# Output projections of both attentions in two halves of the contraction, in a two-layer trunk on one core

## The chip, the cores and the metric

One core of a Trainium2 chip runs the whole program. The metric is the device time of one execution in microseconds (us). The kernel before took 1870.69 us as the median of three runs (1869.51, 1870.69 and 1877.07).

## What is computed

Two layers, each a macaron: half a SwiGLU feed-forward, an attention, half a SwiGLU feed-forward, every one behind an RMS norm and added to the stream x (512 tokens x 1024). Layer 0 has a stick-breaking attention with 16 heads of 64, layer 1 a sliding-window attention with 16 query heads, 2 key heads and sinks. What the change touches is the end of each attention:

```python
x = x + stick_breaking_attention(h, sb_w_in, sb_w_out)
x = x + sliding_window_attention(h, positions, sw_w_in, sw_w_out, q_gain, k_gain, sinks)
...
    return o @ w_out          # o: 512 x 1024 (16 heads of 64), w_out: 1024 x 1024
```

## The kernel before, in words

The stream is kept transposed in SBUF as eight tiles `x0` to `x7` of 128 features x 512 tokens. Everything on TensorE is done in split precision: each operand is a rounded high part and a low part (`oh`, `ol` and so on), and one product of a 128x128 weight tile with a 128x512 operand is three matmuls (`terms`, L214). Such a group of three is called a term below. All TensorE instructions have line 85, since one wrapper records them; the tile names tell them apart. (So have VectorE's where it is held in program order.)

Weights come from DRAM in units of 512 KB (eight 128x128 tiles). SyncE issues the load into a `raw` buffer (L296, three buffers), ScalarE casts it to the high part (L345) and VectorE subtracts to get the low part (L350) into a `slot` (three buffers; a feed-forward has two more of each, `rawx` and `slotx`). `queue` sets the order of the units, and `pump` starts the next load or split when `used` has counted a slot's eight tiles down to zero.

The order of an attention is written by hand. `_Filler` (L101) is a generator of steps with a cost; `fill.run(cost)` between the small steps of a head pair puts that much matmul work there. The amounts are tables: `FILL` and `RATE` for the first attention (L41, one RATE a head pair, two more for its end), `WFILL` and `WRATE` for the second. TensorE keeps the order in which it is written; VectorE and ScalarE are reordered by a scheduler when the program is built, except in the first units of a feed-forward, where `order(True)` holds VectorE in program order too.

The filler of an attention first makes queries, keys and values, then turns to `project_early` (L800): three output tiles of the projection are opened, each in a PSUM bank of the `mm` ring (three banks), and each takes the next head pair's output as soon as it is there (`settled`). An output tile needs all eight 128-row parts of `o`, so the banks and the three weight slots under them stay taken until the last head pair is through. When the last scores are done, a fourth tile is opened in a PSUM bank that has come free; its weights are split into two old query or key tiles (`spare`, `advance`, L355; in the trace `qsw` and `ksw`, or `qw`). `project_out` (L819) finishes the open tiles and does the other four; after each, `residual` (L474) adds it to `x` on VectorE, and `norm_tile` prepares the next feed-forward: a cast on ScalarE (`xh`, L432), a subtraction on VectorE (`xl`, L433), a square on ScalarE, and its sum in `acc` on GpSimd or, for the last two, VectorE (L441). After tile 3 of the first attention `rope_tables` (L886) puts some fifty small VectorE instructions and a sine and a cosine on ScalarE between them.

The feed-forward behind it starts with `plain` (L499). TensorE goes through unit 0 (`gu`, eight terms, one for each x tile); then come the row sums (`ss`, `norm_rows`, with a chain of small VectorE steps that ends in `nr`), unit 1, and the broadcast of the norm (`bc`, `norm_bcast`), whose operand `dg` ScalarE makes from `nr` (L468). The sums of x for the later products (`xg` L506, `t` and its cast L513) are made by ScalarE and VectorE beside it.

## Time and profile before

| | |
|---|---|
| median of three runs | 1870.69 us |
| profiled execution, its whole time | 1871.98 us |
| profiled execution, span | 1870.2 us |
| instructions | 29257 |
| mean granted TensorE clock | 0.989 |
| VectorE busy | 1503.5 us (80%) |
| ScalarE busy | 938.3 us (50%) |
| GpSimd busy | 98.6 us (5%) |
| DMA | 170.94 MB, mean 91 GB/s |
| first attention's projection, first to last matmul | 570.3 to 629 us |
| second attention's projection, first to last matmul | 1426.2 to 1518 us |

Times in the profile are counted from the start of the span. In a row of the timeline the first number is the start, the second the time from there to the row's end, and a bracket at the end gives the idle time of the engine just ahead and what ended it. In a row of the windows view, each engine has its busy time and, in brackets, its instructions; the third number from the end is the granted TensorE clock as a share of full speed.

### The profile page before, as it was taken

To read this page: it belongs to the slowest core of one execution; us is meant where nothing else is said; L and a number is where in the kernel's file an instruction comes from. 1 tells how busy PE (TensorE), PEld (TensorE's weight loads), DVE (VectorE), ACT (ScalarE), POOL (GpSimd) and SP (SyncE) were. 2 spreads that over 40 slices of the span, in tenths; PEclk is the share of its full clock that TensorE was granted. 3 is DMA by queue.
4 is the path that set the end of the run, shared out by engine and by line. 5 is a ranking of instruction groups with operands and counts; after the bars stand their busy time and mean duration, and the time that the engine had idled before them with its cause. 6 is when DMAs were issued, how large, how long until landed. Compare 5 with 4: busy or idle time off the path is not lost.

```text
span 1870.2 us, 29257 instructions
## 1 busy us (share of the span) xinstructions
PE 1827.5 (98%) x11730; PEld 1646.9 (88%) x11730; DVE 1503.5 (80%) x2450; ACT 938.3 (50%) x1497; POOL 98.6 (5%) x83
## 2 busy tenths in 40 slices
PE   7999999999999999999999999999999999999999
PEld 5999999878887789999988999999887788999997
DVE  8888888668987988888869888787688588888884
ACT  6444444456765644444446444444457564444441
POOL 1000000100000100000010000000252210000000
PEclk8999999999999999999999999999999899999999
DMA  5333333221121332333323233322220043333331
GB/s 169 102 102 102 102 102 102 71 77 57 57 68 37 133 101 91 113 94 109 97 74 120 96 100 104 113 92 91 72 68 25 12 134 102 102 102 102 102 102 57
DMA packets 48808, 170.94 MB, mean 91 GB/s; under 512 B 5792, under 2 KB 6048, under 8 KB 48672
## 3 DMA queue, kind: packets, MB, share of 16 engines
q1 hardware_dynamic: 48672, 169.07, 28.3%
q8 instruction: 92, 1.51, 0.3%
q14 instruction: 44, 0.36, 0.1%
HBM read 166.96 MB, written 2.10 MB: 90 GB/s over the span
## 4 chain that ended last, share of the span: by engine, by line
PE 81%; DVE 11%; ACT 4%; issue 3%; POOL 1%; DMA 0%; SPq 0%; ACTq 0%; POOLq 0%; DVEq 0%
PE dn L85 25%; PE a L85 23%; PE c L85 11%; PE b L85 6%; PE tok L85 3%; PE op L85 3%; PE gu L85 3%; DVE keep L732 1%; PE pv L85 1%; DVE t L85 1%; PE q L85 1%; PE k L85 1%; DVE slot L350 1%; PE z L85 1%; PE sc L85 1%
## 5 line engine op out<-in xcount | busy, mean ns | idle before, releaser
L85 PE MATMUL dn<-hs,slot 128*128 128x512 f32 x1152 | 279.1, 391 | 0.0
L85 PEld LDWEIGHTS dn<-hs,slot 128*128 128x128 f32 x1152 | 211.1, 188 | 40.3
L85 PE MATMUL dn<-hs,slotx 128*128 128x512 f32 x960 | 234.2, 392 | 3.3 <-DVE hs L85 1.8
L345 ACT CAST slot<-raw 128x1024 fp32r<-128x1024 f32 (+1 forms) x155 | 160.0, 1033 | 147.0 <-PE a L85 55.2
L85 PE MATMUL a<-t,slot 128*128 128x256 f32 x1728 | 230.2, 283 | 0.0
L85 PEld LDWEIGHTS a<-t,slot 128*128 128x128 f32 x1728 | 222.7, 191 | 6.6
L85 PEld LDWEIGHTS dn<-hs,slotx 128*128 128x128 f32 x960 | 175.5, 188 | 38.4 <-ACT hs L482 2.7
L350 DVE TENSOR_TENSOR slot<-raw,slot 128x1024 fp32r<-128x1024 f32 (+1 forms) x141 | 173.8, 1234 | 16.4 <-ACT slot L345 16.4
L474 DVE SCALAR_TENSOR_TENSOR x<-dn,x 128x512 f32<-128x512 f32 x192 | 131.8, 687 | 44.8 <-PE dn L85 44.7
L85 PEld LDWEIGHTS a<-t,slotx 128*128 128x128 f32 x1008 | 131.1, 191 | 5.3
L85 PE MATMUL a<-t,slotx 128*128 128x256 f32 x1008 | 134.2, 283 | 0.0
L85 PE MATMUL b<-xh,half 128*128 128x256 f32 x608 | 121.9, 283 | 0.0
L441 POOL TENSOR_TENSOR acc<-acc,sq 128x512 f32<-128x512 f32 x30 | 44.9, 1496 | 1313.3 <-ACT sq L440 1313.3
L85 PE MATMUL tok<-slot,xh 128*128 128x256 f32 x576 | 110.9, 292 | 0.1
L85 PEld LDWEIGHTS b<-xh,half 128*128 128x128 f32 x608 | 100.4, 192 | 0.0
L345 ACT CAST slotx<-raw 128x1024 fp32r<-128x1024 f32 x64 | 66.8, 1050 | 64.9 <-PE a L85 56.7
L345 ACT CAST slot<-rawx 128x1024 fp32r<-128x1024 f32 x60 | 63.1, 1052 | 69.4 <-PE a L85 43.3
L85 PE MATMUL c<-xh,slot 128*128 128x256 f32 x480 | 96.2, 283 | 0.0
L85 PEld LDWEIGHTS tok<-slot,xh 128*128 128x128 f32 x576 | 89.9, 192 | 3.3 <-issue 1.1
L553 DVE TENSOR_TENSOR g<-c,r 128x256 f32<-128x256 f32 x76 | 32.3, 424 | 74.7 <-PE c L85 74.1
L85 PE MATMUL gu<-xh,slot 128*128 128x512 f32 x256 | 86.3, 408 | 3.8 <-ACT slot L345 1.9
L547 ACT COPY r<-a 128x256 f32<-128x256 f32 x152 | 56.1, 369 | 65.2 <-PE a L85 64.7
(360 smaller groups left out, 4149.3 us busy)
## 6 DMA issues: line engine op xcount, KB each, us to landing
raw<-in_w_dram SPq DMA_DIRECT2D x165, 512.0 KB, 3.5
rawx<-in_w_dram SPq DMA_DIRECT2D x96, 512.0 KB, 3.5
raw<-in_sbqk_dram SPq DMA_DIRECT2D x16, 512.0 KB, 3.5
raw<-in_swin_dram SPq DMA_DIRECT2D x10, 512.0 KB, 3.5
raw<-in_sbv_dram SPq DMA_DIRECT2D x8, 512.0 KB, 3.5
raw<-in_sbo_dram SPq DMA_DIRECT2D x8, 512.0 KB, 3.5
raw<-in_swo_dram SPq DMA_DIRECT2D x8, 512.0 KB, 3.5
x<-in_xt_dram SPq DMA_DIRECT2D x8, 256.0 KB, 5.2
```

The source lines that it names most:

```text
L85: return self._tc.keep_in_program_order(method(*args, **kwargs))
L345: nc.scalar.copy(hi, src)
L350: nc.vector.tensor_sub(lo, src, hi)
L441: (nc.gpsimd if k < POOL_SQUARES else nc.vector).tensor_add(self.acc, self.acc, sq)
L474: self.nc.vector.scalar_tensor_tensor(self.x[n], ps, factor, self.x[n], ALU.mult, ALU.add)
L547: nc.scalar.copy(r, ps)
L553: nc.vector.tensor_add(g[:, W2:], ps, self.cells["r6", f])
L732: nc.vector.tensor_tensor_scan(rev, rev, rev, 1.0, ALU.mult, ALU.bypass)
```

## The change

The contraction of the output projection is cut in two. `opened` now goes through sixteen half tiles: with parts 0 to 3 of `o` all eight output tiles, each added to `x` at once, then with parts 4 to 7 all eight again, with a second addition and then the norm. `project_early` retires a first-half tile as soon as its four terms are done and opens the next, so three are open until the second half is reached; the extra PSUM bank is taken only then. A unit of `w_out` is laid out as two output tiles x four parts, in the order of use, and no unit is split into old query tiles any more. `residual` thus runs 16 times an attention and not 8; matmuls, weight loads and DMAs are as many as before. Three fill rates are other numbers: RATE for the last head pair 0.54 to 0.95, two of WRATE 1.0 and 0.76 to 1.3 each.

```diff
-RATE = (1.05, 1.05, 1.1, 1.06, 1.05, 1.05, 0.99, 0.54, 1.46, 4.8)
+RATE = (1.05, 1.05, 1.1, 1.06, 1.05, 1.05, 0.99, 0.95, 1.46, 4.8)
...
-WRATE = (1.79, 0.32, 0.71, 0.75, 1.46, 1.0, 0.76, 1.88, 2.19, 2.26)
+WRATE = (1.79, 0.32, 0.71, 0.75, 1.46, 1.3, 1.3, 1.88, 2.19, 2.26)
...
+    def open_out(self, opened, bank=None):
+        h, n = divmod(self.outs, KD)
+        self.outs += 1
+        opened.append([h, n, self.bank("op") if bank is None else bank, self.take(HALF), 0])
+
+    def project_terms(self, t, parts, last):
+        h, n, ps, w, at = t
+        for k in range(at, last):
+            t[4] = k + 1
+            yield from self.terms(ps, [(w[k], parts[h * HALF + k])], first=(k == 0), last=(k == HALF - 1))
...
-            if self.spare and len(opened) == UNITS:
-                bank, tiles = self.spare()
-                self.advance(*tiles)
-                opened.append([bank, self.take(KD), 0])
-            ready = [t for t in opened if t[2] < self.settled]
+            if self.spare and opened[0][0]:
+                self.open_out(opened, self.spare())
+                self.spare = None
+            ready = [t for t in opened if t[4] < min(HALF, self.settled - t[0] * HALF)]
...
+            yield from self.project_terms(t, parts, t[4] + 1)
+            if t[0] == 0 and t[4] == HALF:
+                self.residual(t[1], t[2], 1.0)
+                opened.remove(t)
+                self.open_out(opened)
...
     def project_out(self, parts, opened, following):
+        while opened or self.outs < 2 * KD:
+            if not opened:
+                self.open_out(opened)
+            t = opened.pop(0)
+            for _ in self.project_terms(t, parts, HALF):
+                pass
+            h, n = t[:2]
+            self.residual(n, t[2], 1.0)
+            if h:
+                following(n)
+            if h and n == UNITS and not self.roped:
                 self.rope_tables()
...
-                    net.queue(aps["sbo"][n], special=(n == UNITS))
+                    net.queue(aps["sbo"][n])
...
+    a["sbo"] = c(np.asarray(sb_w_out).reshape(2, HALF, P, HALF, 2, P).transpose(0, 3, 2, 4, 1, 5)).reshape(KD, P, KD * P)
```

What this does to the order is seen at three places. The first is ScalarE in the feed-forward behind the first attention, up to the norm's diagonal `dg`. Before:

```order
L506 ACTIVATE xg<-x_111,gain 128x512
L506 ACTIVATE xg<-x_112,gain 128x512
L345 CAST half_6416<-rawx_6240 128x512
L345 CAST slot_6291<-raw_6221 128x1024
L468 ACTIVATE dg<-ident,nr 128x128 x4
```

And now (line 960 is line 942 of before, the sine of the rope tables):

```order
L345 CAST half_6431<-rawx_6255 128x512
L345 CAST slot_6306<-raw_6236 128x1024
L960 ACT_TABLE_LOAD
L960 ACTIVATE sin<-ang 128x4x8
L962 ACTIVATE cos<-t 128x4x8
L506 ACTIVATE xg<-x_113,gain 128x512
L506 ACTIVATE xg<-x_114,gain 128x512
L345 CAST slot_6358<-rawx_6250 128x1024
L513 CAST t_6319<-t 128x1024
L513 CAST t_6329<-t 128x1024
L468 ACTIVATE dg<-ident,nr 128x128 x4
```

The rope tables, two `xg`, a weight cast and two casts of `t` now stand ahead of `dg`; before, all of these but the rope's, which had run earlier, stood behind it. On TensorE `bc` is where it was, right behind unit 1.

The second place is ScalarE in the last head pair of the first attention, where the values of the pair ahead (`pv`) are folded. Before:

```order
L726 ACTIVATE keep<-z 128x2x384
L790 COPY fold<-pv 64x512
L728 ACTIVATE beta<-z 128x2x384
L790 COPY fold<-pv 64x512
L754 CAST wt_5781<-tr 128x4x128
```

Now:

```order
L726 ACTIVATE keep<-z 128x2x384
L345 CAST slot_5754<-raw_5452 128x1024
L728 ACTIVATE beta<-z 128x2x384
L790 COPY fold<-pv 64x512 x2
L754 CAST wt_5799<-tr 128x4x128
```

A weight cast, which the earlier release of the slot brings here, and `beta` now stand ahead of the first fold.

The third place is TensorE late in the second attention, from the end of one block's values (`pv`) through the transposes of its probabilities (`ptr`) to the next scores (`sc`). Before:

```order
L85 MATMUL pv<-ph,v 128x256
L85 MATMUL ptr<-ident,e 128x128 x4
L85 MATMUL sc<-kh_13436,qs_14534 128x256 x2
L85 MATMUL sc<-kl_13437,qs_14534 128x256 x2
L85 MATMUL sc<-kh_13436,qs_14596 128x256 x2
L85 MATMUL sc<-kl_13437,qs_14596 128x256 x2
L85 MATMUL pv<-ph,v 128x256
```

Now:

```order
L85 MATMUL pv<-ph,v 128x256
L85 MATMUL ptr<-ident,e 128x128 x4
L85 MATMUL op<-oh_14222,slot_14367 128x512
L85 MATMUL op<-ol_14223,slot_14367 128x512
L85 MATMUL op<-oh_14222,slot_14367 128x512
L85 MATMUL op<-oh_13860,slot_14665 128x512
L85 MATMUL op<-ol_13861,slot_14665 128x512
L85 MATMUL op<-oh_13860,slot_14665 128x512 x2
L85 MATMUL op<-ol_13861,slot_14665 128x512
L85 MATMUL op<-oh_13860,slot_14665 128x512
L85 MATMUL op<-oh_14222,slot_14665 128x512
L85 MATMUL op<-ol_14223,slot_14665 128x512
```

Projection matmuls now stand between transposes and scores, where none stood. Over the whole window stage 40 of the 64 terms are ahead of the last `pv`, and 24 were; in the first attention 27 are ahead of the last pair's `pvs`, and 18 were.

More of the change, by code (lines that the diff above doesn't have):

```diff
@@ L814, in project_early @@
             t = ready[0]
[L815 to L825 removed]
+            yield from self.project_terms(t, parts, t[4] + 1)
[3 more added lines that the diff above has]
+                self.open_out(opened)
+    def project_out(self, parts, opened, following):
+        while opened or self.outs < 2 * KD:
+            if not opened:
+                self.open_out(opened)
+            t = opened.pop(0)
[6 more added lines that the diff above has]
+            if h and n == UNITS and not self.roped:
                 self.rope_tables()
@@ L847, in spare @@
             def spare():
[L848 to L849 removed]
+                return self.psum.tile([P, T], F32, tag="pv", name="op", bufs=1)
             for p in range(PAIRS):
@@ L1168, in spare @@
             def spare():
-                tiles = [ap.tile([P, KD * P], F32R, tag="q", name="qw", bufs=2) for _ in range(2)]
-                return self.psum.tile([P, 2, T], F32, tag="z", name="op", bufs=1)[:, 0, :], tiles
+                return self.psum.tile([P, 2, T], F32, tag="z", name="op", bufs=1)[:, 0, :]
             for u in range(CHUNKS * TB + 4):
```

21 lines of the change are left out of this document (4 added, 17 removed).

## The prediction

> **What bounds the kernel now.** I read the page's busy shares first, then TensorE's waits in the two stretches that the change touches, then the granted clock there.
>
> ```profile
> PE 1827.5 (98%) x11730; PEld 1646.9 (88%) x11730; DVE 1503.5 (80%) x2450; ACT 938.3 (50%) x1497; POOL 98.6 (5%) x83
> ```
>
> TensorE is busy for 98% of the span and the change takes no matmul away. So it can only win back time in which TensorE stands still, or runs slowly. The waits of TensorE, first from 560 to 680 us (last head pairs, projection, start of the next feed-forward), then from 1426 to 1520 us (the second attention's end); columns are total us, times, longest:
>
> ```profile
> PE pv L85 <- DVE o L791: 2.9, 1, 2.9
> PE gu L85 <- ACT xh L432: 1.7, 1, 1.7
> PE dn L85 <- ACT hs L482: 0.8, 1, 0.8
> PE dn L85 <- DVE hs L85: 0.7, 1, 0.7
> PE gu L85 <- DVE xl L433: 0.5, 1, 0.5
> ```
>
> ```profile
> PE pv L85 <- DVE pl L1104: 2.5, 4, 1.3
> PE ptr L85 <- DVE pl L1104: 1.9, 1, 1.9
> PE qtr L85 <- DVE pl L1104: 1.4, 1, 1.4
> PE qtr L85 <- DVE hf L975: 0.5, 1, 0.5
> PE op L85 <- ACT oh L1113: 0.5, 1, 0.5
> ```
>
> That is 6.6 us and 6.8 us of standing still. The clock adds to the second (the windows view; the number after POOL's is the granted clock):
>
> ```profile
> 1445.00:1450.00 5.00, 4.51 (x20) 3.80 (x18) 4.91 (x15) 3.73 (x11) 1.56 (x1) 0.66 0.13 23
> 1450.00:1455.00 5.00, 3.58 (x15) 2.93 (x16) 3.76 (x15) 3.12 (x10) 1.77 (x2) 0.70 0.22 85
> 1455.00:1460.00 5.00, 5.00 (x25) 4.73 (x25) 2.02 (x9) 3.08 (x11) 1.50 (x2) 0.62 0.00 0
> 1470.00:1475.00 5.00, 3.67 (x16) 3.04 (x16) 3.88 (x17) 4.09 (x15) 1.76 (x2) 0.74 0.00 2
> 1475.00:1480.00 5.00, 5.00 (x29) 4.28 (x28) 1.72 (x4) 2.21 (x7) 2.82 (x2) 0.91 0.02 3
> ```
>
> Five times (1 - clock) gives 1.7 + 1.5 + 1.9 = 5.1 us lost to a lower clock in the first three rows and 1.3 + 0.45 = 1.75 us in the last two. Each dip stands right behind a wait:
>
> ```profile
> 1444.74 0.78 PE L85 MATMUL qtr<-ident,q 128*128 128x128 f32 x4 [1.42 <-DVE pl L1104]
> 1451.41 0.66 PE L85 MATMUL ptr<-ident,e 128*128 128x128 f32 x4 [1.90 <-DVE pl L1104]
> 1471.47 0.39 PE L85 MATMUL pv<-pl,v 128*128 128x256 f32 x1 [1.33 <-DVE pl L1104]
> ```
>
> So what can be won is 6.6 us at the first attention and 6.8 + 6.85 us at the second, 20 us or 1.1% at the very most.
>
> **The change part by part.** One term and one addition cost:
>
> ```profile
> 604.91 0.39 PE L85 MATMUL op<-o4h,qsw 128*128 128x512 f32 x1
> 605.59 0.39 PE L85 MATMUL op<-o5h,qsw 128*128 128x512 f32 x1
> L474 DVE SCALAR_TENSOR_TENSOR x<-op,x x16: 674/684/692, 603.7 to 1518.3; 128x512 f32<-128x512 f32 x16
> ```
>
> A term is 605.59 - 604.91 = 0.68 us of TensorE. An addition is 0.68 us of VectorE; eight more in each attention are 5.5 us there, none of it on TensorE unless a bank or a later VectorE step waits. Splits of weights, DMAs and SyncE's issues are as many as before and in the same order; they move earlier, into the last head pairs, where the slots now come free.
>
> *Second attention.* Before, three tiles times four finished parts are 12 terms; then the filler is empty, and TensorE goes from values to transposes to scores with nothing between (the third place in the order). Now 32 first-half terms are there. The wait of 1.42 at 1444.74 and the dip behind it (a third of the first 5.1, 1.7) stay: the order up to there is the same. Before 1451.41 there is one term more (0.68), and the split into `qw` on VectorE (1.2 by its neighbours of the same size) is gone from ahead of `pl`: 1.90 becomes 0.3, so -1.6, and the two dip stretches behind it go, 5.1 - 1.7, so -3.4. At 1471.47 three to four terms stand ahead: -1.3, and its dip, -1.75. Against this: the last two transposes have no term between them any more (+0.7, a term), and 5.5 us of additions and three more weight splits fall into the stretch on VectorE. VectorE is 3.76 and 2.02 of 5 us busy in the rows 1450 to 1460, so most of it fits; I take +0.8, with ends of 0 and 4.0 (the three waits above, put back). Sum: -1.6 - 3.4 - 1.3 - 1.75 + 0.7 + 0.8 = -6.6 us.
>
> *First attention, last head pair.* The wait of 2.9 is for the fold of the pair ahead; its rows:
>
> ```profile
> 577.53 1.50 PE L85 MATMUL pv<-wt,v 128*128 128x512 f32 x8
> 579.40 0.81 ACT L726 ACTIVATE keep<-z 128x768 f32<-128x768 f32 x1 [2.26 <-DVE beta L733]
> 580.84 0.81 ACT L728 ACTIVATE beta<-z 128x768 f32<-128x768 f32 x1
> 582.68 1.51 PE L85 MATMUL pv<-wt,v 128*128 128x512 f32 x8 [2.90 <-DVE o L791]
> ```
>
> More filler is ahead of the first `pv` (two terms, 1.36 us), but ScalarE now has a weight cast (about 1.0) and `beta` (0.81) between `keep` and the fold, and VectorE a split and `beta` ahead of `o` (about 2.0 together). 2.9 + 2.0 - 1.36 is 3.5: the wait stays, +0.6. Ends: -2.9 (gone) and +2.0 (nothing of the filler helps).
>
> *Behind it.* After the last part `o7` TensorE has 29 terms left and not 46 less the seven that cover it, so it reaches the feed-forward with 9 terms (6.1 us) less for VectorE to do the additions, `xl` and rope in. VectorE has less to do there too: two splits (2.4) and some nineteen rope steps (0.16 each, 3 us) have moved away, one addition has come. The wait for the last x tile, 1.7 + 0.5, stays about as it is; I take -0.4, ends -2.2 and +1.5.
>
> *The gate `bc`.* This is the large one. TensorE must run `bc` behind unit 1, in order. Its operand `dg` now stands on ScalarE behind the rope's sine and cosine, two `xg`, a weight cast and two casts of `t`, and those wait for VectorE. The rows of before:
>
> ```profile
> 637.63 1.05 PE L85 MATMUL ss<-ones,acc 128*128 128x1 f32 x8
> 644.12 1.02 PE L85 MATMUL bc<-dg,ones 128*128 128x512 f32 x2
> 641.94 0.16 DVE L85 SCALAR_TENSOR_TENSOR nr<-nt,nr 128x4 f32<-128x4 f32 x1
> 642.02 1.23 DVE L85 TENSOR_TENSOR slot<-raw,slot 128x1024 fp32r<-128x1024 f32 x1
> 643.16 0.75 DVE L85 TENSOR_TENSOR t<-xg 128x256 f32<-128x256 f32 x2
> 643.83 0.88 DVE L85 SCALAR_TENSOR_TENSOR t<-t,xg 128x256 f32<-128x256 f32 x2
> 642.20 1.28 ACT L468 ACTIVATE dg<-ident,nr 128x128 f32<-128x128 f32 x4 [0.44 <-DVE nr L85]
> 633.12 0.22 ACT L944 ACTIVATE cos<-t 128x32 f32<-128x32 f32 x1
> 638.25 1.33 ACT L506 ACTIVATE xg<-x,gain 128x512 f32<-128x512 f32 x2
> 647.17 1.04 ACT L345 CAST slot<-rawx 128x1024 fp32r<-128x1024 f32 x1
> 645.22 2.04 ACT L513 CAST t<-t 128x1024 fp32r<-128x1024 f32 x2
> ```
>
> Before, `dg` starts 0.1 us after `nr` is done (642.1) and ends at 643.48; `bc` follows at 644.12 without a wait, 0.6 us of slack. Now, counted from the end of `nr`: VectorE first does the split (1.2) and then the rope step that the cosine waits for (0.2), so the cosine ends at 1.6; the two `xg` end at 2.9, the weight cast at 3.9, the casts of `t` at 5.9 (VectorE's eight short steps for them, twice 0.75 and twice 0.88, are done by about 4.7), `dg` at 7.2. That is 5.8 us later than the 1.4 of before. The chain to `nr` is also about 0.6 later against `ss`, since rope steps are woven into it, which uses up the slack. So TensorE waits 5.8 us: +5.8, ends 4.0 (the casts of `t` close up and TensorE arrives later) and 7.5 (a load lands late).
>
> Such a wait cools the clock too. The first feed-forward has one of 10 us:
>
> ```profile
> 45.06 0.80 PE L85 MATMUL gu<-xh,slotx 128*128 128x512 f32 x1 [10.01 <-DVE g L85]
> 40.00:50.00 10.00, 4.94 (x13) 3.91 (x14) 8.21 (x14) 4.13 (x5) 0.00 (x0) 0.55 0.05 12
> ```
>
> At 0.55 over ten microseconds 4.5 are lost, of which about 2.5 fell on the wait itself (40 to 45.06 at half): 2 us of matmuls ran slow behind it. I take +1.9 here. In return VectorE and ScalarE get 5.8 us ahead, and the `dn` waits of 0.8 + 0.7 later in this feed-forward shrink: -0.8. Sum of the first attention: +0.6 - 0.4 + 5.8 + 1.9 - 0.8 = +7.1 us.
>
> The skill has a rule on these dips. The Trainium skill, "TensorE: Matmul & The Clock Gate", section "Part 1: The HAM clock gate", says that the clock falls to half after one idle window of about 3.4 us and comes back after one busy one. By that rule waits of 1.33 to 1.90 us would cool nothing, and the three dips would have another cause and stay; the rows above, each dip right behind such a wait, speak against it, so the sum goes by the rows.
>
> Together: -6.6 + 7.1 = +0.5 us. The profiled execution took 1871.98 us (1.8 more than its span), 1.3 more than the median of the three runs, 1870.69. So 1872.5 for such an execution, 1871 for the median.
>
> **The rivals.**
>
> *The gate is hidden* (the change is worth what its words promise). If VectorE reaches the last x tile late enough, TensorE is late at `bc` as well, or the casts of `t` are long done, and neither the 5.8 nor the 1.9 is paid, nor the 0.8 won: -6.6 + 0.6 - 0.4 = -6.4, 1864 us. For it: TensorE already waits 2.2 us for that x tile. Against it: `ss` and `nr` hang on the same tile, so `bc`'s lateness is counted from there, whoever is late. Chance 0.2.
>
> *VectorE becomes the bound of the second attention's end* (slower). The rows 1445 to 1450 have it at 4.91 of 5 us; two additions stand there now just ahead of `pl`, and `pl` is what TensorE waits for. If each costs its wait again, 1.9 and 1.3 come back with their dips, and the second attention gives 0 to +1, so the first's +7.1 stands alone: 1878 to 1879 us, and over 1880 if `bc` takes its upper end. It decides once VectorE has no free microsecond between scores and `pl`. Against it: from 1455 us on the rows above have VectorE at 2.02 to 3.88 of 5 us. Chance 0.17.
>
> *The clock doesn't follow waits as short as these.* Only a standstill as long as the 10 us one would cool it, and the three dips come from elsewhere and stay. Filling then wins 1.6 + 1.3 and pays 0.7 + 0.8, so -1.4, and the first attention's +7.1 stays: 1876 us. The three dips right behind three waits speak against it. Chance 0.08. (This is what the Trainium skill, "TensorE: Matmul & The Clock Gate", "Part 1: The HAM clock gate", would have.)
>
> *The filler only changes places*, every wait moves with it, and neither gain nor gate shows: 1870.7. Chance 0.05; the order on ScalarE speaks against it.
>
> **How the numbers follow.** The forecast has 0.5. Its own range is the sum of likely errors, 1867 to 1876. The range reaches from 1862 (the hidden gate with a further clock stretch won) to 1878 (VectorE the bound). About 0.5%, 9.4 us, is what a measurement of this kernel can tell from no change. Below 1861 lies a third of the hidden gate and little else, 0.12; above 1880 a good half of the VectorE rival and the tails of two others, 0.13; within, 0.75.
>
> **What would show it.** In the new profile: a wait of `bc` for `dg` of 4 to 7.5 us some 15 us after the first attention's last projection matmul, with a clock near 0.5 behind it; the 2.9 us wait for `o` still there; in the second attention no dip at what was 1452 to 1459 and 1472 to 1476 us, and its first scores-to-projection stretch 5 to 8 us shorter. No wait at `bc` proves the first attention's sum wrong; dips that stay with the waits gone prove my reading of the clock wrong.

## The result and the profile after

The kernel with the projections in halves takes 1887.1 us (median; 1884.0 to 1887.9 over four executions), the kernel before 1872.1 us beside it (1869.5 to 1877.1). The ratio is 1.0062, 95% interval 1.0044 to 1.0080; that is 11.6 us, while the two medians, of four executions each, lie 15.0 us apart. The forecast was 1871.0 us, with a range from 1862 to 1878: the measured median lies 9 us above its upper end. The profiled execution of after took 1884.01 us, the least of its four, with a span of 1882.2 (before: 1871.98 and 1870.2), so the two profiles lie 12.0 us apart and hold most of the difference.

First TensorE's share, the page's first row of after:

```profile
PE 1832.4 (97%) x11730; PEld 1647.9 (88%) x11730; DVE 1509.5 (80%) x2466; ACT 938.3 (50%) x1497; POOL 99.0 (5%) x83
```

The matmuls are as many as before, and VectorE has the sixteen additions more (2466 against 2450, 6.0 us more busy time). Next, TensorE's timeline in the first attention's last pair and in the feed-forward behind it:

```profile
583.69 2.60 PE L85 MATMUL pv<-wt,v 128*128 128x512 f32 x8 [3.00 <-DVE o L791]
637.52 0.50 PE L85 MATMUL gu<-xh,slot 128*128 128x512 f32 x1 [0.88 <-ACT xh L432]
638.85 0.50 PE L85 MATMUL gu<-xl,slot 128*128 128x512 f32 x1 [0.83 <-DVE xl L433]
652.08 2.08 PE L85 MATMUL bc<-dg,ones 128*128 128x512 f32 x2 [4.21 <-ACT dg L468]
```

The fold's wait is there as before, the waits for the last x tile are 1.71 together instead of 2.22, and `bc` has a new wait of 4.21. The `dn` waits (0.84 and 0.71 before) have no row any more. The granted clock there, from the windows view (third number from the end):

```profile
580.00:590.00 10.00, 7.00 (x23) 5.54 (x23) 5.13 (x8) 3.14 (x6) 0.00 (x0) 0.66 0.17 52
640.00:650.00 10.00, 7.88 (x31) 6.08 (x30) 8.98 (x40) 6.77 (x11) 0.00 (x0) 0.83 0.57 184
650.00:660.00 10.00, 7.92 (x20) 5.62 (x21) 9.83 (x16) 8.97 (x14) 0.00 (x0) 0.66 0.00 0
```

Ten times (1 - clock) is 3.4 us behind the fold and 1.7 + 3.4 = 5.1 us around `bc`; before, all three windows had 1.00. The 1.7 lies ahead of `bc`'s wait: the clock is 0.50 from 641.2 to 644.6, behind the two waits for the x tile, and again from 651.5 to 658.3.

Now the second attention, the same two views:

```profile
1450.82 0.39 PE L85 MATMUL pv<-ph,v 128*128 128x256 f32 x1 [0.51 <-ACT ph L1121]
1451.79 0.39 PE L85 MATMUL pv<-pl,v 128*128 128x256 f32 x1 [0.58 <-DVE pl L1122]
1455.79 0.36 PE L85 MATMUL pv<-ph,v 128*128 128x256 f32 x1 [0.83 <-DVE st L1100]
1456.71 0.38 PE L85 MATMUL pv<-pl,v 128*128 128x256 f32 x1 [0.56 <-DVE pl L1122]
1496.60 0.39 PE L85 MATMUL pv<-pl,v 128*128 128x256 f32 x1 [1.87 <-DVE pl L1122]
```

```profile
1450.00:1460.00 10.00, 7.52 (x39) 5.89 (x38) 8.42 (x30) 7.71 (x23) 3.79 (x2) 0.85 0.00 0
1460.00:1470.00 10.00, 10.00 (x60) 8.30 (x58) 7.33 (x23) 6.52 (x23) 2.69 (x1) 0.98 0.16 54
1490.00:1500.00 10.00, 8.13 (x41) 6.80 (x41) 6.01 (x10) 5.25 (x14) 1.89 (x1) 0.90 0.18 58
1500.00:1510.00 10.00, 8.96 (x51) 7.16 (x50) 2.83 (x5) 2.41 (x5) 0.00 (x0) 0.93 0.00 0
```

The wait of 1.42 at 1444.74 that the forecast let stand, and those of 1.90 and 1.33 that it wanted to take away, have no counterpart any more. In their place TensorE has several short ones (0.51 + 0.58 + 0.83 + 0.56 = 2.48 between 1450 and 1457) and a late one of 1.87 in front of the last values. The clock loses 1.5 + 0.2 + 1.0 + 0.7 = 3.4 us in these windows; in the forecast's rows of before it was 6.85.

The place that no term of the forecast named is behind it, the start of the last feed-forward. TensorE's timeline there, of before and of after: its first product, the norm's column sums `ss`, and the second of its blocks of sums:

```profile
1518.07 0.39 PE L85 MATMUL gu<-xh,slot 128*128 128x512 f32 x1
1523.51 0.95 PE L85 MATMUL ss<-ones,acc 128*128 128x1 f32 x8
1573.38 0.28 PE L85 MATMUL b<-xh,half 128*128 128x256 f32 x1
```

```profile
1525.36 0.39 PE L85 MATMUL gu<-xh,slot 128*128 128x512 f32 x1
1533.69 1.05 PE L85 MATMUL ss<-ones,acc 128*128 128x1 f32 x8
1585.38 0.28 PE L85 MATMUL b<-xh,half 128*128 128x256 f32 x1
```

From the first product to that block it is 55.31 us before and 60.02 after: 4.71 us given back in the same work. The waits that make it up, after:

```profile
1530.06 0.50 PE L85 MATMUL gu<-xl,slot 128*128 128x512 f32 x1 [0.22 <-DVE xl L433]
1532.31 0.49 PE L85 MATMUL gu<-xh,slot 128*128 128x512 f32 x1 [1.51 <-ACT xh L432]
1533.09 0.50 PE L85 MATMUL gu<-xl,slot 128*128 128x512 f32 x1 [0.29 <-DVE xl L433]
1573.29 0.50 PE L85 MATMUL dn<-hs,slotx 128*128 128x512 f32 x1 [1.70 <-ACT hs L482]
1574.98 0.72 PE L85 MATMUL dn<-hs,slotx 128*128 128x512 f32 x2 [1.19 <-DVE hs L85]
```

Before, the first three have no wait at all, and the `dn` pair waits less (TensorE's timeline of before):

```profile
1561.62 0.51 PE L85 MATMUL dn<-hs,slotx 128*128 128x512 f32 x1 [0.32 <-ACT hs L482]
1562.97 0.73 PE L85 MATMUL dn<-hs,slotx 128*128 128x512 f32 x2 [0.84 <-DVE hs L85]
```

From the first product to where TensorE is ready for the `dn` pair it is 43.23 us before and 46.23 after. So 3.0 us are lost at `gu` (2.0 in brackets, the rest where each wait breaks up the stream of products) and 1.7 at `dn`.

For `gu` the reason is on VectorE. Its timeline behind the last values, a few rows of after (the brackets give idle time; none of these rows has one):

```profile
1512.57 0.74 DVE L433 SCALAR_TENSOR_TENSOR xl<-x,gain,xh 128x512 fp32r<-128x512 f32 x1
1513.93 1.22 DVE L350 TENSOR_TENSOR slot<-raw,slot 128x1024 fp32r<-128x1024 f32 x1
1517.44 2.31 DVE L350 TENSOR_TENSOR slot<-raw,slot 128x1024 fp32r<-128x1024 f32 x1
1521.82 0.68 DVE L474 SCALAR_TENSOR_TENSOR x<-op,x 128x512 f32<-128x512 f32 x1
1526.10 1.77 DVE L433 SCALAR_TENSOR_TENSOR xl<-x,gain,xh 128x512 fp32r<-128x512 f32 x1
1530.53 0.68 DVE L474 SCALAR_TENSOR_TENSOR x<-op,x 128x512 f32<-128x512 f32 x1
```

and of before, the last two additions to x:

```profile
1512.83 0.69 DVE L474 SCALAR_TENSOR_TENSOR x<-op,x 128x512 f32<-128x512 f32 x1 [2.38 <-PE op L85]
1518.27 0.69 DVE L474 SCALAR_TENSOR_TENSOR x<-op,x 128x512 f32<-128x512 f32 x1 [1.86 <-PE op L85]
```

Before, VectorE waits for TensorE ahead of the last two tiles, and the last addition starts 0.20 us after the feed-forward's first product (1518.27 against 1518.07). After, the last addition starts 5.17 us after it (1530.53 against 1525.36): VectorE is behind. A second-half tile needs 12 matmuls where a whole one needed 24, so finished x tiles come at twice the pace, and each costs an addition, `xl` and, for most, the split of a weight (for the last two also a square's sum).

For `dn` the rows point to ScalarE, which makes `g` and from it, by way of VectorE's `h`, the operand `hs`. ScalarE's order is set when the program is built, and here, some 40 us behind the changed code, it has come out another way. Before, `g` runs ahead of the cast into `slotx`:

```profile
1558.79 0.64 ACT L492 ACTIVATE g<-g 128x512 f32<-128x512 f32 x1
1560.01 1.05 ACT L345 CAST slotx<-raw 128x1024 fp32r<-128x1024 f32 x1 [0.58 <-PE c L85]
```

After, it runs behind the cast and behind the cast's wait for TensorE's products `c`:

```profile
1570.28 1.05 ACT L345 CAST slotx<-raw 128x1024 fp32r<-128x1024 f32 x1 [1.11 <-PE c L85]
1571.23 0.63 ACT L492 ACTIVATE g<-g 128x512 f32<-128x512 f32 x1
```

In the experiments below every kernel with `g` behind that cast waits 1.7 + 1.19 at `dn`, and every kernel with `g` ahead of it waits 0.32 + 0.84.

All parts together, each from a start on TensorE to the next (before, then after): up to the norm behind the first feed-forward 375.37 and 376.03; from there to the next feed-forward's first product 254.02 and 255.68; from there to its second block of sums 58.65 and 65.18; on to the window stage's norm 644.99 both; from there to the last feed-forward's first product 185.04 and 183.48; its start 55.31 and 60.02; the rest 296.8 both. The differences are +0.66, +1.66, +6.53, 0, -1.56, +4.71 and 0, which is the 12.0. The +0.66 is not the change's: the code there is the same, and over all kernels below it takes 374.6 to 376.6.

The second attention can be cut once more. TensorE's order is the same in both kernels from the window stage's norm up to the term ahead of the transposes that waited 1.90 (1449.1 in before, 1460.6 in after). Cut at that term's last product, the 185.04 and 183.48 are 116.09 + 68.94 before and 118.70 + 64.78 after: 2.61 us are lost where TensorE's order is unchanged, and 4.16 are won behind it.

### The profile page after: what moved, and what is told of

It reads as the page before. It is cut to its first block, busy times and chain, and to the rows that moved or that the text cites. A ratio compares the mean times of both kernels' runs of the same rounds, so it can differ in the third digit from the quotient of the medians.

```text
span 1882.2 us, 29276 instructions
## 1 busy us (share of the span) xinstructions
PE 1832.4 (97%) x11730; PEld 1647.9 (88%) x11730; DVE 1509.5 (80%) x2466; ACT 938.3 (50%) x1497; POOL 99.0 (5%) x83
## 4 chain that ended last, share of the span: by engine, by line
PE 82%; DVE 9%; ACT 4%; issue 3%; POOL 1%; DMA 0%; SPq 0%; ACTq 0%; DVEq 0%; POOLq 0%
PE dn L85 25%; PE a L85 23%; PE c L85 11%; PE b L85 6%; PE gu L85 4%; PE tok L85 3%; PE op L85 3%; PE pv L85 1%; DVE slot L350 1%; DVE keep L732 1%; PE q L85 1%; PE k L85 1%; PE sc L85 1%; DVE t L85 1%; ACT slot L345 1%
## 5 line engine op out<-in xcount | busy, mean ns | idle before, releaser
L350 DVE TENSOR_TENSOR slot<-raw,slot 128x1024 fp32r<-128x1024 f32 (+1 forms) x143 | 178.6, 1250 | 17.6 <-ACT slot L345 17.5
## 6 DMA issues: line engine op xcount, KB each, us to landing
x<-in_xt_dram SPq DMA_DIRECT2D x8, 256.0 KB, 5.5
```

The lines of the kernel that those rows point to most:

```text
L350: nc.vector.tensor_sub(lo, src, hi)
```

## The experiments

Theory "gate": the loss is TensorE's wait for the norm's diagonal `dg` behind the first attention, with the clock it costs. Its rival "VectorE": the additions make VectorE late everywhere. A third, "pace", came up behind the first four runs: the finished x tiles come faster than VectorE can take them.

Each ratio is to the kernel before on the same chip, with its 95% interval. The stretches are those of the sum above, read from one profiled execution each; "clock" is how much of a stretch went to a granted clock below 1, summed as length times (1 - clock) over windows of 2 us.

| kernel | ratio | first attention (clock) | start of the FFN behind it (clock) | second attention (clock) | start of the FFN behind it (clock) |
|---|---|---|---|---|---|
| before | 1 | 254.0 (1.7) | 58.65 (0) | 185.0 (10.2) | 55.31 (0) |
| after | 1.0062 [1.0044, 1.0080] | 255.7 (3.4) | 65.18 (5.1) | 183.5 (6.9) | 60.02 (0) |
| e1 first only | 1.0039 [1.0027, 1.0051] | 256.0 (3.4) | 65.45 (5.1) | 185.2 (10.2) | 55.32 (0) |
| e2 second only | 1.0034 [1.0022, 1.0046] | 254.1 (1.7) | 59.21 (1.7) | 186.3 (10.2) | 60.03 (0) |
| e3 after, `dg` first | 1.0043 [1.0029, 1.0057] | 256.0 (3.4) | 60.91 (1.7) | 183.4 (6.9) | 60.03 (0) |
| e4 after, rope early | 1.0021 [1.0012, 1.0030] | 258.3 (3.4) | 54.73 (0) | 181.8 (5.1) | 64.74 (5.1) |
| e5 second only, no first additions | 1.0042 [1.0027, 1.0057] | 256.9 (5.1) | 60.67 (3.4) | 181.1 (5.1) | 64.76 (5.1) |
| e6 second only, old rates | 1.0036 [1.0023, 1.0048] | 255.7 (3.4) | 60.63 (3.4) | 184.3 (8.5) | 64.72 (5.1) |
| e7 before, rope early | 0.9982 [0.9971, 0.9993] | 253.3 (0) | 54.73 (0) | 183.8 (6.8) | 55.33 (0) |
| e8 first only, rope early | 0.9985 [0.9974, 0.9995] | 258.4 (3.4) | 54.73 (0) | 181.3 (5.1) | 55.32 (0) |
| e9 second only, no squares | 0.9990 [0.9980, 1.0000] | 256.9 (5.1) | 60.64 (3.4) | 183.4 (6.8) | 55.31 (0) |
| e10 before, no squares | 0.9996 [0.9984, 1.0009] | 256.9 (5.1) | 60.63 (3.4) | 184.8 (8.5) | 55.31 (0) |
| e11 after, rope early, no squares | 0.9967 [0.9954, 0.9980] | 258.2 (3.4) | 54.71 (0) | 186.5 (10.2) | 55.34 (0) |
| e12 before, rope early, no squares | 0.9977 [0.9968, 0.9987] | 254.9 (1.7) | 54.70 (0) | 185.4 (8.5) | 55.33 (0) |
| e13 second only, sums on VectorE | 1.0020 [1.0008, 1.0032] | 254.1 (1.7) | 59.17 (1.7) | 182.7 (5.1) | 59.70 (1.7) |
| e14 second only, sums on GpSimd | 1.0023 [1.0014, 1.0032] | 254.1 (1.7) | 60.60 (3.4) | 180.9 (3.4) | 62.19 (3.4) |
| e15 after, rope early, sums on VectorE | 0.9997 [0.9986, 1.0008] | 258.6 (5.1) | 54.73 (0) | 180.8 (3.4) | 58.19 (0) |

### Each attention alone (e1, e2)

e1 takes the change's code for the first attention and the old code, weight layout and rates for the second; e2 the other way round. The core of it, e1:

```diff
 # sliding_window
-                yield from self.project_early(parts, opened)
+                yield from self.whole_early(parts, opened)
...
-            self.project_out(parts, opened, following)
+            self.whole_out(parts, opened, following)
```

> Only the first attention's projection is in two halves, the second is as before. From the two profiles I place +9.7 us at the first attention and the feed-forward behind it and +3 us at the second. Both theories, the one of the gate (the wait of the norm's broadcast for its diagonal, with the clock stretches behind it) and the one of VectorE (eight more additions make it late everywhere), expect 8 to 12 us more than before, near 1882. If the loss were in the second attention, this would be within 3 us of before.

> Only the second attention's projection is in two halves, the first is as before. From the profiles +3 us (2 to 6), near 1875: 1.5 us won up to the last projection matmul and 4.7 us given back in the feed-forward behind it. The prediction's own sum would have -6.6 us. If the second attention's loss comes only from what the first one shifts (its clock stretches fall elsewhere), this would be at or below before.

Measured: 1.0039 and 1.0034, about +7 and +6 us at the 1875.3 us of the kernel before on that chip. The first attention's +7.3 us (0.39% of 1875) is near the forecast's +7.1; for the 9.7 of e1's expectation the stretches above give 1.66 + 6.53 = 8.2. The second, forecast at -6.6, loses by itself, and twice the 3 us that e2's expectation took from the profiles. The two sum to 1.0073, within the interval of the full change: they are separate losses, and the table shows where each sits, e1's in the first feed-forward start (65.45), e2's in the last (60.03).

### The first attention's gate (e3, e4, e7, e8)

e3 writes the four steps of `dg` on ScalarE right behind the norm's rows; e4 computes the rotary tables behind the fourth first-half tile. e7 and e8 carry e4's idea to a kernel with no halves (in the last head pair there) and to one with the first attention in halves only:

```diff
 # e3, behind norm_rows() of the first attention's feed-forward
+                if self.stage == "1":
+                    self.norm_diagonal()
 # e4 and e8, project_early
                 self.residual(t[1], t[2], 1.0)
+                if t[1] == UNITS and not self.roped:
+                    self.rope_tables()
 # e7, stick_breaking of before
+                    if p == PAIRS - 1 and i == TB - 2:
+                        self.rope_tables()
```

> The changed kernel with the norm's diagonal written right behind the row sums in the feed-forward after the first attention, so that ScalarE does it ahead of the casts of t. Theory of the gate: the wait of 4.2 us falls below 1.5 us and the clock stretch behind it goes, 5 to 7 us less than the changed kernel, near 1881. Theory of VectorE: the work on VectorE is the same, at most 2 us less, 1885 or more.

> The changed kernel with the rope tables made in the last head pair, behind the fourth first-half tile, and not behind the fourth second-half tile. Theory of the gate: the same as moving the diagonal, 5 to 7 us less than the changed kernel, and the wait for the last x tile (1.7 us) goes too, so up to 9 us less, near 1879. Theory of VectorE: fifty small steps (8 to 10 us) now fall into the last head pair, where VectorE is already late with the fold; what is won behind it is lost there, within 3 us of the changed kernel.

> The kernel before, with the rotary tables computed in the first attention's last head pair and not between its output tiles. Theory "gate": the tables' instructions on VectorE and ScalarE lie ahead of the next FFN's norm only in the kernel with halves, where PE comes sooner to it; here nothing waits for them, so 1873.5 to 1878 beside 1875.3. Rival: they cost the kernel before as well (waits for its last split x tiles at the gate), and it gains 2 to 5 us.

> Only the first attention in halves, and the rotary tables behind its fourth first-half tile. Theory "gate": the first attention's loss (7.3 us with halves alone) is the gate's waits and the clock behind them; with the tables out of the way it goes, and moving them gave 7.7 us in the full change, so 1873 to 1876. Theory "VectorE": the eight additions cost something of their own, 1877 to 1881.

e3: `bc`'s wait is gone and the start falls from 65.18 to 60.91 us, 3.4 of it in the clock. In time (1883.2 us, ratio 1.0043) it lies between the two expectations. Part comes back: the work that `dg` passed now ends later, and TensorE waits for `g`. TensorE's timeline of e3:

```profile
660.04 0.50 PE L85 MATMUL gu<-xh,slotx 128*128 128x512 f32 x1 [0.68 <-DVE g L85]
```

The `dn` waits, gone in after, are back with 0.68 and 0.92 (0.84 and 0.71 before).

e4 removes the cause and not the order: the start takes 54.73 us with every clock window at full speed, and the ratio drops from 1.0062 to 1.0021 (1879.1 us, as the theory of the gate had it). The tables cost something where they now stand: behind three new waits (0.85, 0.22 and 0.84) the first attention takes 258.3 us.

e7 missed its first expectation and met its rival: without any halves, early tables win 0.18% (interval 0.07 to 0.29%), because the start behind the first attention falls from 58.65 to 54.73 us there too. So the tables cost the kernel before as well. That leaves e8 to be read against e7 and not against before: 0.9985 and 0.9982 (its 1871.7 us came out below both its expectations). With the tables away, halves in the first attention neither win nor lose anything that can be measured. The gate theory stands for the first attention.

### The second attention: additions and rates (e5, e6)

```diff
 # e5: project_early, second attention only in halves
             if t[0] == 0 and t[4] == HALF:
-                self.residual(t[1], t[2], 1.0)
                 opened.remove(t)
 # e6
-WRATE = (1.79, 0.32, 0.71, 0.75, 1.46, 1.3, 1.3, 1.88, 2.19, 2.26)
+WRATE = (1.79, 0.32, 0.71, 0.75, 1.46, 1.0, 0.76, 1.88, 2.19, 2.26)
```

> Only the second attention in halves, with the eight additions of its first-half tiles to x left out (its output lacks those halves). Theory "additions": the eight additions of 0.69 us lie between the value products' subtractions and splits on VectorE, and make VectorE's results late; then the second attention in halves costs nothing without them, 1873 to 1877 beside the 1882.2 of the kernel with only the second attention halved. Theory "pace": the time goes where the eight finished x tiles come at the double pace (12 products apart where there were 24) and with less of the projection left behind the last value product; the additions count for little, and it stays at 1880 to 1884, with the same short waits of PE and the same waits at the next FFN's start.

> Only the second attention in halves, with the filling rates of the kernel before (1.0 and 0.76 at the two places where the change has 1.3 and 1.3). Theory "rates": the higher rates use the filling up before the last value products and leave 24 products behind them where there were 40; with the old rates some 8 to 16 products more are left, the next FFN's start waits less, and it takes 1876 to 1880. Theory "pace": the rates only move waits from one place of the attention to another, 1881 to 1885, and the waits at the next FFN's start stay within 1 us.

Measured: 1.0042 and 1.0036, beside 1.0034 for e2. The 1882.3 us of e5 lie in the range of "pace", the 1880.2 of e6 between its two. The last feed-forward's start is 64.7 us in both, 60.0 plus some 4.7 us that go with half-clock windows which e2's execution didn't have; its five waits are those of e2 within 0.02 us. So neither the eight additions nor the two rates make the loss there, and theory "VectorE" in its first form (the additions) falls.

Two limits. In e6 four terms moved later within the attention, but still 40 of the 64 are ahead of the last `pv` and 24 behind it, as in e2; the 8 to 16 more of its expectation did not come, so more terms behind the attention were never tried. And inside the attention both edits count for something: the late wait of 1.87 is 1.15 in e5, and 0.65 and 0.34 in e6. The four short waits ahead of it are the same in both.

### The pace of the finished tiles (e9 to e12)

```diff
             nc.scalar.activation(self.acc, self.x[k], AF.Square)
-        else:
+        elif which < 5:
             sq = w.tile([P, T], F32, tag="rbc", name="sq", bufs=1)
```

> Only the second attention in halves; behind it, the squares of x tiles 1 to 7 are left out of the last feed-forward's norm (so its output is not the reference's), which takes five additions of 1.3 to 1.6 us from GpSimd, two of 0.69 us from VectorE, and seven squares from ScalarE. So far every kernel with the second attention in halves takes 60.0 or 64.8 us from the last feed-forward's first product to its second block of sums, every one without takes 55.3, and from the window stage's norm to that first product both take 181 to 186. Theory "pace": the finished x tiles come 2.8 us apart, and VectorE, with additions, splits, weight splits and the slow-down beside GpSimd's additions, needs longer for one; with about 5 us of its work gone the stretch falls to 55.3 to 57, and the time to 1873 to 1878. Theory "inside": the loss of 6 us lies in the attention itself, and the stretch stays near 60 or the time near 1881.

> The kernel before with the same squares left out (its output is not the reference's either). Both theories: there VectorE waits for PE behind its last x tiles, so nothing depends on those squares, the stretch stays at 55.3 us, and the time within 1.5 us of the kernel before.

> The full change, with the rotary tables behind the fourth first-half tile and the same squares left out: both places where time was given back are eased. Theory "pace": what is left is what halves are worth in themselves, and that is nothing that shows beside the kernel before with early tables: 1870 to 1875. Rival: the halves do win some 5 us inside the attentions once nothing behind them takes it back: 1864 to 1868.

> The kernel before with early rotary tables and the same squares left out, to stand beside the one above: as without the squares left out, 1869 to 1873 (1870.6 measured with them).

This is the decisive group. In e9 the start is 55.31 us, to a hundredth what it is in before, and the ratio goes from 1.0034 to 0.9990. Its waits there are before's again, and `gu` has none (TensorE's timeline of e9); ScalarE's order at `dn` is before's too:

```profile
1565.19 0.50 PE L85 MATMUL dn<-hs,slotx 128*128 128x512 f32 x1 [0.31 <-ACT hs L482]
1566.54 0.74 PE L85 MATMUL dn<-hs,slotx 128*128 128x512 f32 x2 [0.84 <-DVE hs L85]
```

In e10 the same work is taken from the kernel before and nothing happens (0.9996, 55.31 us): there it was hidden behind TensorE's matmuls. So the 4.7 us hang on that work behind the attention's end. For the 3.0 at `gu` VectorE's rows show how; for the 1.7 at `dn` it may be no more than ScalarE's order, which e9 put back as well, and no run separates the two. The pace of the tiles and the fewer terms left behind the attention came together in all runs, so these aren't separated either. e11 and e12 ask what is left of the halves with both places eased: 0.9967 [0.9954, 0.9980] against 0.9977 [0.9968, 0.9987], which can't be told apart. The rival's 1864 to 1868 didn't come: e11's 1869.4 us lie between it and the expected 1870 to 1875, and by the two intervals a gain of up to some 5 us from the halves isn't excluded.

### Whose work it is (e13, e14, e15)

```diff
-            (nc.gpsimd if k < POOL_SQUARES else nc.vector).tensor_add(self.acc, self.acc, sq)
+            (nc.gpsimd if k < (0 if which == 5 else POOL_SQUARES) else nc.vector).tensor_add(self.acc, self.acc, sq)
```

The limit is 0 in e13 and e15, and 8 in e14. e15 also has the tables where e7 has them.

> Only the second attention in halves; for the last feed-forward's norm all seven additions of squares are VectorE's (0.69 us each, 3.4 us more for it), none GpSimd's. From the profile of the kernel with only the second attention in halves: beside GpSimd's five additions of 1.3 to 1.6 us, VectorE's splits took 3.7 us more than without. Theory "slow-down": that is the larger half of VectorE's lateness; the waiting for GpSimd's slower additions goes too, and the stretch from the last feed-forward's first product to its second block of sums falls from 60.0 to 56 to 58.5 us. Theory "work": VectorE's own work is what counts, and it has as much as before, so 59.5 to 61, or 64.7 with a clock dip.

> Only the second attention in halves; for the last feed-forward's norm all seven additions of squares are GpSimd's, two more than before. Theory "slow-down": two more additions of 1.3 to 1.6 us slow VectorE's last splits, and the norm's sum comes later, since GpSimd needs twice VectorE's time: 61 to 63 us (64 to 68 with a clock dip) and a time of 1882 to 1885. Theory "work": VectorE loses 1.4 us of work ahead of its last split tile, and the stretch falls to 58 to 59.5.

> The full change, with the rotary tables in the first attention's last head pair and all additions of squares for the last feed-forward's norm on VectorE; its output is the reference's. Halves are worth nothing in themselves by the runs so far, so the most it can do is to stand where the kernel before with early tables stood: 1871 to 1875 if the last feed-forward's start is mended by VectorE's additions, 1876 to 1879 if not.

e13: although VectorE has five more additions to do, `gu`'s three waits vanish; a wait of 0.61 at `ss` is new, and the two `dn` waits stay, with after's order on ScalarE:

```profile
1521.91 1.05 PE L85 MATMUL ss<-ones,acc 128*128 128x1 f32 x8 [0.61 <-DVE acc L441]
1561.82 0.50 PE L85 MATMUL dn<-hs,slotx 128*128 128x512 f32 x1 [1.71 <-ACT hs L482]
1563.51 1.22 PE L85 MATMUL dn<-hs,slotx 128*128 128x512 f32 x2 [1.19 <-DVE hs L85]
```

Its 59.70 us lie in the range of "work", but 1.7 of them are clock; e15, with the same code there and no clock loss, takes 58.19, in the range of "slow-down". So 1.8 us (60.02 - 58.19) come back when GpSimd adds no squares, all of it ahead of `dn`: of the 3.0 us lost there 1.15 are left. The trace of after shows two ways in which those additions hold VectorE up. One is the slower steps of the last section. The other is a queue: the squares share one buffer, so ScalarE's square of 1523.08 waits 0.84 us for GpSimd's addition, a weight's cast stands behind that square, and VectorE's split of 1524.69 waits 1.09 us for the cast. In e13 VectorE has no gap in the same place. The shares of the two aren't separated.

e14's 62.19 lies in the range of "slow-down", but 3.4 of it are clock, and at `dn` it has before's order on ScalarE and before's waits of 0.32 + 0.84. Ahead of `dn` it loses 6.9 us, 3.5 without the clock, where e2 loses 3.0, and its waits at `gu` are 2.91 us for e2's 2.03. So the rows lean to "slow-down"; its 1878.0 us, expected at 1882 to 1885, don't. In times, e13 and e14 (1.0020, 1.0023) lie below e2 with overlapping intervals, so only the stretches tell them apart.

e15 puts both remedies into the full change and lands at 0.9997 (1873.8 us, in the range expected): the loss is undone, and nothing is won. The only kernels with the reference's whole work that beat the kernel before have early tables and the second attention whole: e7 without any halves and e8 with the first attention in halves.

## Why the prediction was wrong

What failed is the sum of the second attention, "Sum: -1.6 - 3.4 - 1.3 - 1.75 + 0.7 + 0.8 = -6.6 us". With the start of the feed-forward behind it, the profiles have -1.56 + 4.71 = +3.15. The 9.7 us between come from three places, with 2.6, 2.4 and 4.7.

First, "the order up to there is the same". On TensorE it is, on VectorE and ScalarE it isn't, and the part ahead of the cut loses 2.61 us for which the forecast has no term. Over all kernels that part takes 114.5 to 117.6 us with whole tiles and 117.2 to 121.7 with halves; without the clock it is 110.8 to 112.0 and 112.9 to 114.0. VectorE does none of the additions there (the first starts at 1461.0, behind the cut) and one split fewer, but otherwise the same steps in another order, and TensorE meets the four short waits of 0.51 to 0.83. Every kernel with halves has them, e5 and e6 among them, and none with whole tiles. Which swap makes which wait stays open.

Second, a size. Behind the cut, where all terms of the sum lie, the gains came, but smaller: -4.16 in the two profiles, and on the mean over all kernels 68.4 us with whole tiles (64.8 to 70.3) against 64.1 with halves (62.6 to 65.3). The wait of 1.90 is gone, but one of 1.87 is new; the brackets there add up to 4.00 before and 2.91 after. Of these 4.3 us, 2.8 are clock and 1.5 are not. The forecast added the waits and the dips as if each had its own price. The same code has that wait at 1.90 us in before and e1, but at 3.48 in e7, e10 and e12: in the first two the clock is low for 3.4 us just ahead of it, TensorE comes to it later, and the wait is 1.6 us shorter. And one profile is a draw: the whole stretch loses 5.1 to 10.2 us to the clock in the six kernels with whole tiles and 3.4 to 10.2 in those with halves.

Third, a term is missing. The forecast costed less filler behind the first attention's last part, with "-0.4", but nothing behind the second attention's, where 24 terms are left in place of 40 and tiles finish at the double pace. That is +4.7 us, or 9.4 when three clock windows fall there as in e4, e5 and e6. e9 and e10 show it.

The first attention's sum held: +7.1 forecast, 1.66 + 6.53 = 8.2 in the profiles, 7.3 by e1's times. That it came so near is partly luck: `bc` was put 1.6 too high and the clock too low, and before's profile is a favourable draw. In the seven other kernels with the same first attention and tables, that attention and the start behind it take 313.3 to 317.6 us, in before 312.7, with halves 320.9 (after) and 321.4 (e1); so the halves cost 3.3 to 8.7 there. The parts, in the forecast's order:

- Fold wait, +0.6: 3.00 after 2.90, so +0.1. The 3.4 us in the clock behind it was not forecast, and isn't the change's: e5, e9 and e10, with the old code there, lose the same (see the last section).
- Last x tile, -0.4: 1.71 after 2.22, so -0.5.
- `bc`, +5.8: 4.21. The chain was sized rightly; ScalarE's timeline of after:

```profile
645.92 0.24 ACT L962 ACTIVATE cos<-t 128x32 f32<-128x32 f32 x1 [1.30 <-DVE t L959]
648.86 1.99 ACT L513 CAST t<-t 128x1024 fp32r<-128x1024 f32 x2
650.75 1.27 ACT L468 ACTIVATE dg<-ident,nr 128x128 f32<-128x128 f32 x4
```

and the last step to `nr` on VectorE:

```profile
644.51 0.16 DVE L85 SCALAR_TENSOR_TENSOR nr<-nt,nr 128x4 f32<-128x4 f32 x1
```

`dg` ends at 652.02, 7.35 us behind the end of `nr` (644.67); forecast 7.2. The wait is shorter because TensorE came later: 1.7 us of 640 to 650 went to the clock.

- Clock behind it, +1.9: 5.1 in that stretch, against none before. But 1.7 of it comes ahead of the wait, and the seven other kernels with the old code lose 1.7 to 3.4 in the same place. Behind the wait it is 3.4 in after, 0.3 of it on the wait itself, and 1.7 in e1, so the term was not far off.
- Later `dn` waits, -0.8: 0.84 + 0.71 = 1.55 are gone altogether.

Of the rivals, "VectorE becomes the bound of the second attention's end" came nearest, with 1878 to 1879 for 0.17. It had the engine, the sign and nearly the worth of that stretch, but not the cause or the place: the additions it named come only behind the cut, e5 without them keeps the short waits, and it did not look at the finished tiles. "The gate is hidden" is excluded by the 4.21. "The clock doesn't follow waits as short as these" named 1876, with a +1.9 that its own condition would take away (1874.5 without); dips do come behind waits of 0.5 to 1.9 us, but not after each and not in each execution.

Of the prediction's own tests, the wait at `bc` was there in the range given (4 to 7.5), the fold's wait too; "what was 1452 to 1459 and 1472 to 1476" is 8.85 us later in after, and the clock is 1.00 there (1461 to 1467 and 1481 to 1485), so these dips are gone; but there is a new one behind the wait of 1.87, from 1498.0 to 1501.4. The stretch behind the cut is 4.2 us shorter, not 5 to 8. No test looked ahead of that stretch or behind it, where the rest was lost.

Two slips in the working changed little: the upper end of 4.0 is +0.8 and two waits (1.90 + 1.33), not three, and 46 less seven is 39, ten terms more than 29 and not nine.

## What to carry to other kernels

Work that a matmul stream hides has a rate, not only a sum: when a change makes results finish in a quicker succession, compare what the other engines do for one result with the new distance between two, to the end of the chain behind them. An edit to the order of one engine can reorder the others where the program is scheduled when it is built: so compare the order of every engine, also ahead of the changed place and well behind it, and look for steps that stand in a queue without need, as the rotary tables stood here. And compare stretches that start and end at the same instruction: where the medians differed by a few parts in ten thousand and no clock was lost, these agreed to 0.03 us or differed by a microsecond and more.

## What the hardware showed

**The clock is lost in quanta.** Every loss in the table is a multiple of 1.7 us within 0.1: half of a stretch of 3.4 us at half speed (in after the granted clock is 0.50 from 641.2 to 644.6 and from 1457.0 to 1460.4). The edges lie on one grid: in before they are 1393.9, 1400.8, 1445.1, 1448.5, 1452.0, 1458.8, 1472.4 and 1475.9, all whole steps of 3.41 us apart. So whether a wait costs one should be a matter of phase. e2 and e5 run the same code up to the second attention and have the same wait for the fold. TensorE's row and the clock in e2:

```profile
582.00 1.49 PE L85 MATMUL pv<-wt,v 128*128 128x512 f32 x8 [2.90 <-DVE o L791]
```

```profile
580.00:590.00 10.00, 8.00 (x48) 6.73 (x48) 7.44 (x12) 5.18 (x10) 0.00 (x0) 1.00 0.00 0
```

and in e5:

```profile
583.37 2.60 PE L85 MATMUL pv<-wt,v 128*128 128x512 f32 x8 [2.90 <-DVE o L791]
```

```profile
580.00:590.00 10.00, 7.10 (x26) 5.89 (x25) 5.06 (x7) 4.37 (x7) 0.00 (x0) 0.66 0.00 0
```

One execution pays 3.4 us and the other nothing, for the same 2.90 us. Laid on each execution's grid, by the profile's ends of matmuls, the wait puts at most 1.5 us of standstill into one step of the grid in e2 and 2.2 in e5. Over the eight kernels with this code the clock fell behind a step with 1.83 us or more (five of them) and not at 1.78 or less (three). That is no rule for other places: elsewhere a step with 0.75 us was followed by a slow one, and one with 1.84 was not. The Trainium skill, "TensorE: Matmul & The Clock Gate", "Part 1: The HAM clock gate", says that activity is watched in a free-running window of 3.4 us and that the clock halves after an idle one; the size of the quantum and the play of phase agree with the free-running window. That a whole window must be idle doesn't agree: the clock fell in e5 behind 2.90 us, less than a window, and in after behind waits that add up to 2.5 us over 6 us (1450 to 1457 above). So a wait's clock cost is an expectation over phases, and one profile shows one draw.

**GpSimd slows VectorE's two-input steps.** GpSimd's timeline of after, its additions of squares:

```profile
1517.05 1.62 POOL L441 TENSOR_TENSOR acc<-acc,sq 128x512 f32<-128x512 f32 x1 [0.74 <-ACT sq L440]
1521.71 1.34 POOL L441 TENSOR_TENSOR acc<-acc,sq 128x512 f32<-128x512 f32 x1 [3.04 <-ACT sq L440]
1525.88 1.44 POOL L441 TENSOR_TENSOR acc<-acc,sq 128x512 f32<-128x512 f32 x1 [0.79 <-ACT sq L440]
```

Beside them VectorE's split of a weight takes 2.31 instead of 1.22 us (1517.44) and `xl` 1.77 instead of 0.74 (1526.10), while the addition of `op` to x, with one operand in PSUM, keeps its 0.68 right inside GpSimd's step (1521.82). In e13, where GpSimd adds no squares, the splits in the same place all take 1.22 and `xl` 0.75. The Trainium skill, "SBUF — State Buffer", "Who interferes with whom", says that a VectorE instruction with two SBUF inputs contends with a GpSimd instruction that reads SBUF, and one with at most one, outside the 2-port perf modes, doesn't; both halves of that agree with these rows. So an addition given to GpSimd is not free for VectorE: 1.3 to 1.6 us there cost up to 1.1 us here, against 0.68 for VectorE doing it itself.
